# Context halves first in the last four pw1 outputs, each inverse transform one output behind its forward one, and SiLU tiles between pw2's first matmuls

## The chip, the cores and the metric

The kernel runs on one core of a Trainium2 chip. The metric is device time in microseconds; the kernel before takes 1690.03 us, the median of three runs (1689.47 to 1690.48). A core has five engines that run their own instruction streams and wait for one another through semaphores: TensorE (PE, matmuls and transposes), VectorE (DVE), ScalarE (ACT), GpSimd (POOL) and SyncE (SP), whose queue issues the weight loads here.

## The reference, cut to what matters

Two layers over 256 latent tokens and 256 context tokens of width 1024. Layer 0, the only one that the change touches, is a Conformer convolution module followed by a squared-ReLU MLP:

```
u  = x*(1+sc1) + sh1                      # sc1, sh1, g1, sc2, sh2, g2: maps of c (latent) or c_ctx
a  = u @ w_pw1 + b_pw1                    # 1024 -> 2048
a  = a[:, :1024] * sigmoid(a[:, 1024:])   # value half times gate half
a  = dwconv(a, w_dw)                      # depthwise, 31 taps; latents in rows of 64, context in one row of 256
a  = silu(layer_norm(a + b_dw))           # norm over the 1024 channels of one token
y  = a @ w_pw2 + b_pw2
h  = layer_norm(ALPHA*x + g1*y)           # LN1
h  = layer_norm(ALPHA*h + g2*sq_relu_mlp(h*(1+sc2)+sh2))
```

## The kernel before, in words

Feature-major tiles hold 128 features by 512 tokens; tokens 0 to 255 are the context (half LO, `s == 0`), 256 to 511 the latents (half HI, `s == 1`). Every fp32 product is made of three matmuls on split operands (`mm3`, lines 177, 180, 181: high by high, high by low, low by high), so a weight tile of 128x1024 is first split by ScalarE (`wh`, L154) and VectorE (`wl`, L155). The split tiles have four buffers each, the raw weights three (`raw_load`, L150, on SP's queue, in order). PSUM has eight banks: three `mm`, two `ln`, two `cv`, one `fl`.

The convolution is done as a transform. pw1's outputs come as m = 0 to 11 after four made earlier: even m is the gate of a feature tile f, odd m its value. `pw1_epi` takes a gate through Sigmoid on ScalarE (L660); for a value VectorE multiplies it in (L663), PE transposes the result (L666) and ScalarE copies it to `A` (L667), tokens on partitions. `spectral(h, tt)` makes channels 512h to 512h+511 of token block tt (0, 1 context, 2, 3 latents): forward matmuls (L683, L688), four VectorE products with the taps' spectrum (`F`, L698 and L699), then after its `yield` the inverse matmuls (L709), the bias (L716) and the statistics (L717). `token_norm(t0)` turns the statistics of blocks t0 and t0+1 into scale and shift by two aggregations and a chain of thirteen tiny VectorE operations (L722, then L507 to L512, L726 and L727) and normalizes four tiles on ScalarE (L731). `silu(s)` then makes eight tiles: two PE transposes (L751), Sigmoid and Identity on ScalarE (L754, L755), product on VectorE (L756), split (L154, L155). pw2 multiplies them; `pw2_epi` adds each output into `x` (L900) and feeds the LN1 sums (`Norm`, L433 to L462).

Beside that run the modulation maps of layer 0. `AdaRows` (`ada0`, 16 steps for g1 and sc2) makes one step of two VectorE row products (L387) on a loaded weight; `Ada` (`ada_sh`, for sh2) uses PE (L327) into the `fl` bank, a copy (L361) and a fold by PE (L335).

The instructions are put in order at build time by a scheduler that takes, engine by engine, the first ready instruction in the order of the program; those marked by `keep_in_program_order` (while `pin[0]` is true) keep their order among themselves. Before the change, m = 0 to 9 are made over 512 tokens and only m = 10, 11 in halves; the sequence around them is

```
10c 11c 10x(epi 11c) | fwd0 | 11x first half | fwd1 | 11x second half | inv0 | epi 11x | inv1
token_norm(0) | fwd2 | ada | inv2 | fwd3 | ada | inv3 | fold | silu(0) | token_norm(2) | pw2: m 0-3 kt by kt, m 4-7
```

with c and x for the context and the latent half. Then pw2 runs over the latents while `silu(1)` supplies its tiles, two for each output of the context half.

Of the kernel before, what the change touches and what calls it, by code (L numbers as in the profile page):

```python
# [72 lines left out]
def hybrid_kernel(ctx: ExitStack, tc: tile.TileContext, xT, vecs_d, rows_d, wdw_d, ada0_w, ada_w, adar_w, wg_d, pw1a, pw1, pw2, w1_0, w2_0,  # L73
# [28 lines left out]
    def psum(tag="mm"):  # L102
        return pp.tile([P, 512], F32, tag=tag, name=nm(tag), bufs={"mm": 3, "ln": 2, "fl": 1, "cv": 2}[tag])
# [44 lines left out]
    def raw_load(src):  # L148
        raw = wp.tile([P, 2048], F32, tag="raw", name=nm("raw"), bufs=3)
        nc.sync.dma_start(raw[:, :src.shape[-1]], src)  # L150
        return raw
# [113 lines left out]
        for _ in gemm2_steps(*a, **k):  # L265
            pass

    def gemm2_steps(w_ap, groups, rhs, order, epi, keep, ko=0, pre=None):


        ws = dict(pre or {})
        raws = {}

        def weights_of(m):
            if m not in ws:
                g = groups[m // 2]
                if g not in raws:
                    raws[g] = raw_load(w_ap[g, 0])
                ws[m] = split_w(raws[g][:, (m % 2) * 1024:(m % 2 + 1) * 1024], keep if m >= NW else None)
            return ws[m]  # L280

        for i, (s, sl) in enumerate(order):
            r = [(h_[:, sl], l_[:, sl]) for h_, l_ in rhs] if not isinstance(rhs, dict) else rhs[s]
            k0 = ko if i == 0 else 0
            if k0:
                pss = [psum("mm" if m < 3 else "cv")[:, :C] for m in range(k0)]
                for m in range(k0):
                    weights_of(m)
                for kt in range(8):
                    for m in range(k0):  # L290
                        mm3(pss[m], *kcol(ws[m], kt), *r[kt], kt == 0, kt == 7)
                for m in range(k0):
                    epi(m, pss[m], s, sl)
                yield
            for m in range(k0, 2 * len(groups)):
                w = weights_of(m)
                ps = psum()[:, :C]
                for kt in range(8):
                    mm3(ps, *kcol(w, kt), *r[kt], kt == 0, kt == 7)
                epi(m, ps, s, sl)  # L300
                yield
# [115 lines left out]
    class Norm:  # L417

        def __init__(self, n, bufs):
            self.n, self.ts, self.i = n, [], 0
            self.acc, self.k, self.s2 = bufs

        def add(self, t, pin=False):
            self.ts.append(t)
# [84 lines left out]
            nc.vector.scalar_tensor_tensor(q, q, 0.5, v, op0=ALU.mult, op1=ALU.mult)  # L511
            nc.vector.scalar_tensor_tensor(r, q, -1.5, r, op0=ALU.add, op1=ALU.mult)  # L512

    def norm_pair(make):

        b = [make() for _ in range(3)]
        return [Norm(C, [t[:, sl] for t in b]) for sl in (LO, HI)]

    def affine_half(hi, lo, src, s, ca, cb, f):

# [224 lines left out]
    def silu(s):  # L745
        for f in range(DT):
            if f % 2 == 0:
                tr = psum("ln")
            xn = tr[:, f % 2 * C:f % 2 * C + C]
            for i in range(2):  # L750
                nc.tensor.transpose(xn[:, i * P:(i + 1) * P], Y[2 * s + i][f // 4][:, f % 4 * P:f % 4 * P + P], ident)  # L751
# [3 lines left out]
            nc.scalar.activation(y, xn, AF.Identity, scale=V("cln_g", f), bias=V("cln_b", f))  # L755
            nc.vector.tensor_tensor(y, y, sg, op=ALU.mult)  # L756
            t = U(F32R)
            split(t[:, LO], t[:, HI], y)
            sact[s].append((t[:, LO], t[:, HI]))
            yield  # L760

    ada0, ada_sh = AdaRows(0, (2, 4)), Ada(6, 2)
    gb = con.tile([P, 2, DT], F32, name="gb")

    def pw1_next(m, ps):
        pw1_epi(m + KO0, ps)
        if m == 4:
            for tt in range(4):
                for _ in spectral(0, tt):
                    pass  # L770
        ada0.step((1, 2, 1, 2, 2, 2, 2, 2, 1, 1)[m])
        if m == 5:
            for s, sl in HALVES:
                nc.vector.tensor_tensor(gb[:, s, :], ad(0, s, "g1"), VA("b_pw2"), op=ALU.mult)
                for f in range(DT):
                    nc.vector.tensor_scalar(x[f][:, sl], x[f][:, sl], ALPHA, gb[:, s, f:f + 1], op0=ALU.mult, op1=ALU.add)
        if m == 7:
            taps(1)

    nc.sync.dma_start(cb, c_dr.rearrange("(o s c) -> o s c", o=1, s=2).broadcast_to([P, 2, D]))  # L780
    steps = gemm_steps(pw1, range(5), u, T, pw1_next)
    next(steps)

    bdw = padp.tile([P, D], F32, name="bdw")
# [50 lines left out]
    raw = raw_load(pw1[5, 0])
    wl2 = [split_w(raw[:, m * D:(m + 1) * D]) for m in range(2)]
    ps2 = [psum() for _ in range(2)]

    def pw1_part(m, s, kts=range(DT)):
        sl = HALVES[s][1]  # L840
        for kt in kts:
            mm3(ps2[m][:, sl], *kcol(wl2[m], kt), *[t_[:, sl] for t_ in u[kt]], kt == 0, kt == DT - 1)

    def part_epi(m, s):
        pw1_epi(10 + m + KO0, ps2[m], 2 * s, 2 * s + 2)

    pin[0] = True
    for m in range(2):
        pw1_part(m, 0)
        if m == 0:  # L850
            part_epi(0, 0)
    pw1_part(0, 1, range(4))
    part_epi(1, 0)
    pw1_part(0, 1, range(4, DT))
    part_epi(0, 1)
    pre_pw2(0)
    sp = [spectral(1, tt, banks=("mm", "fl")) for tt in range(2)]
    next(sp[0])
    pw1_part(1, 1, range(4))
    next(sp[1])  # L860
    pw1_part(1, 1, range(4, DT))
    for _ in sp[0]:
        pass
    part_epi(1, 1)
    for _ in sp[1]:
        pass
    normed = token_norm(0)
    pre_pw2(1)
    for tt in (2, 3):
        sp1 = spectral(1, tt, normed)  # L870
        next(sp1)
        ada_sh.mm()
        for _ in sp1:
            pass
    ada_sh.end()
    pin[0] = False
    for _ in silu(0):
        pass
    token_norm(2)
    close_pool()  # L880
    hp = open_pool("hidp")
    HD = maker(hp, "hid", 2 * DT)
    lnp = norm_pair(maker(hp, "ln", 3))
# [15 lines left out]
    def pw2_epi(m, ps, s, sl):  # L899
# [876 lines left out]
```

## Time and profile before

| | |
|---|---|
| median of three runs | 1690.03 us |
| the profiled execution's own time | 1691.92 us |
| its span on the core | 1690.2 us |
| mean granted TensorE clock | 0.996 |
| PE busy | 1660.0 us (98%) |
| DVE busy | 1091.3 us (65%) |
| ACT busy | 745.5 us (44%) |
| DMA queue of the weight loads | 285.44 MB, 46.5% of 16 engines |

Times inside the profile count from the start of the span. A row of the timeline gives an instruction's start, its length, engine, line, operation, output and inputs, and in brackets the idle time of that engine just before it with what ended it. Rows by windows give busy time by engine, then the granted TensorE clock, the share of the DMA engines and GB/s. Successive PE matmuls overlap by their pipeline, so the distance from start to start is what one costs.

### The profile page before, as it was taken

The page shows a single profiled execution, that of the slowest core. Times are in us where ns is not written, and L with a number is a line of the kernel's source. Part 1 is how long each engine was busy: PE and PEld are TensorE (multiplying, and loading weights), DVE is VectorE, ACT ScalarE, POOL GpSimd, SP SyncE. Part 2 cuts the span into 40 slices and gives each one's busy share as a digit, 9 for nine tenths or more (in the row PEclk, how much of TensorE's full clock was granted, in tenths as well). Part 3 has the DMA queues.
Part 4 walks back from the last instruction along what each step waited for, and adds up shares of the span by engine and source line. Part 5 has one row for each costly group of instructions (what it writes and reads, how often), then busy time and mean ns, then how long its engine had stood idle before and what let it go on. Part 6 is the DMA issues. An engine that isn't in the chain of part 4 may idle for free.

```text
span 1690.2 us, 22717 instructions
## 1 busy us (share of the span) xinstructions
PE 1660.0 (98%) x8853; PEld 1366.5 (81%) x8853; DVE 1091.3 (65%) x1964; ACT 745.5 (44%) x1206; POOL 33.5 (2%) x84
## 2 busy tenths in 40 slices
PE   8998999999999999999999999999999999999998
PEld 5765997888888998876688899888877878888886
DVE  7996896976666786763232543453387786678765
ACT  3322763232324465552232532442376574555652
POOL 0000000000000000000000000000011110000000
PEclk9999999999999999999999999999999999999999
DMA  9534216565545055567653632344355555645651
GB/s 387 206 128 181 95 51 224 199 224 199 198 176 200 26 183 171 186 222 280 232 187 108 213 143 100 113 161 150 117 193 188 189 195 207 244 171 216 246 181 47
DMA packets 60669, 301.60 MB, mean 178 GB/s; under 512 B 6067, under 2 KB 20947, under 8 KB 27153
## 3 DMA queue, kind: packets, MB, share of 16 engines
q1 hardware_dynamic: 42832, 285.44, 46.5%
q10 hardware_dynamic: 17728, 14.70, 2.6%
q8 instruction: 70, 1.15, 0.3%
q14 instruction: 39, 0.31, 0.1%
HBM read 284.37 MB, written 15.75 MB: 178 GB/s over the span
## 4 chain that ended last, share of the span: by engine, by line
PE 88%; DVE 7%; ACT 3%; issue 1%; DMA 1%; POOL 0%; SPq 0%; DVEq 0%; ACTq 0%; POOLq 0%
PE mm L177 17%; PE mm L180 16%; PE mm L181 16%; PE mm L192 4%; PE mm L1599 3%; PE mm L187 3%; PE mm L185 3%; PE mm L186 3%; PE mm L196 2%; DVE wl L155 2%; PE cv L186 2%; PE cv L187 2%; PE cv L185 2%; PE mm L1600 2%; PE fl L820 1%
## 5 line engine op out<-in xcount | busy, mean ns | idle before, releaser
L155 DVE TENSOR_TENSOR wl<-raw,wh 128x1024 fp32r<-128x1024 f32 x346 | 421.7, 1223 | 301.9 <-ACT wh L154 299.1
L154 ACT CAST wh<-raw 128x1024 fp32r<-128x1024 f32 x346 | 360.4, 1050 | 479.8 <-PE mm L180 282.4
L180 PE MATMUL mm<-u,wh 128*128 128x512 f32 (+1 forms) x832 | 297.8, 359 | 1.0 <-DVE u L533 0.5
L177 PE MATMUL mm<-u,wh 128*128 128x512 f32 (+1 forms) x704 | 249.7, 357 | 2.2 <-ACT wh L154 2.2
L181 PE MATMUL mm<-u,wl 128*128 128x512 f32 (+1 forms) x704 | 246.8, 352 | 0.8 <-DVE wl L155 0.8
L180 PEld LDWEIGHTS mm<-u,wh 128*128 128x128 f32 x832 | 158.0, 190 | 24.8 <-issue 1.8
L177 PEld LDWEIGHTS mm<-u,wh 128*128 128x128 f32 x704 | 133.1, 190 | 27.2 <-issue 5.1
L181 PEld LDWEIGHTS mm<-u,wl 128*128 128x128 f32 x704 | 133.7, 190 | 20.2 <-DVE wl L155 1.4
L177 PE MATMUL mm<-xm,wh 128*128 128x512 f32 x256 | 102.8, 402 | 0.0
L185 PE MATMUL mm<-wh,xl 128*128 128x512 f32 x256 | 101.3, 397 | 0.7 <-ACT wh L154 0.5
L186 PE MATMUL mm<-wh,xl 128*128 128x512 f32 x256 | 100.5, 392 | 0.6 <-DVE xl L155 0.6
L181 PE MATMUL mm<-xm,wl 128*128 128x512 f32 x256 | 100.3, 392 | 0.0
L187 PE MATMUL mm<-wl,xl 128*128 128x512 f32 x256 | 99.7, 394 | 0.2 <-DVE wl L155 0.2
L387 DVE CUSTOM_DVE_ANT_0 raw<-raw,cb,vecs 128x1024 f32<-128x1024 f32 x64 | 81.5, 1280 | 28.5 <-DMA raw<-adar_w 27.9
L177 PE MATMUL mm<-hid,wh 128*128 128x512 f32 (+1 forms) x256 | 93.2, 364 | 0.0
L180 PE MATMUL mm<-hid,wh 128*128 128x512 f32 (+1 forms) x256 | 92.9, 363 | 0.0
L181 PE MATMUL mm<-hid,wl 128*128 128x512 f32 (+1 forms) x256 | 92.9, 363 | 0.0
L1599 PE MATMUL mm<-x,wh 128*128 128x512 f32 x224 | 79.0, 397 | 0.0
L180 PE MATMUL mm<-qq,wh 128*128 128x272 f32 x256 | 73.9, 289 | 0.0
L177 PE MATMUL mm<-qq,wh 128*128 128x272 f32 x256 | 73.5, 288 | 0.0
L181 PE MATMUL mm<-qq,wl 128*128 128x272 f32 x256 | 73.5, 288 | 0.0
L192 PE MATMUL mm<-u,wh 128*128 128x512 f32 x192 | 68.4, 398 | 0.0
(498 smaller groups left out, 3288.8 us busy)
## 6 DMA issues: line engine op xcount, KB each, us to landing
raw<-w SPq DMA_DIRECT2D x64, 1024.0 KB, 4.9
raw<-adar_w SPq DMA_DIRECT2D x32, 1024.0 KB, 4.8
raw<-wo SPq DMA_DIRECT2D x32, 1024.0 KB, 4.8
raw<-ada_w SPq DMA_DIRECT2D x16, 1024.0 KB, 6.3
raw<-wv SPq DMA_DIRECT2D x16, 1024.0 KB, 5.4
raw<-wqT SPq DMA_DIRECT2D x16, 1024.0 KB, 5.2
raw<-wq SPq DMA_DIRECT2D x16, 1024.0 KB, 4.8
raw<-wk SPq DMA_DIRECT2D x16, 1024.0 KB, 4.8
```

The costliest lines, as they stand in the source:

```text
L154: c = nc.scalar.copy(hi, src)
L155: nc.vector.tensor_tensor(lo, src, hi.bitcast(F32), op=ALU.subtract)
L177: a = nc.tensor.matmul(ps, wh, xh, start=start, stop=False)
L180: nc.tensor.matmul(ps, wh, xl, start=False, stop=False)
L181: nc.tensor.matmul(ps, wl, xh, start=False, stop=stop)
L185: nc.tensor.matmul(ps, xh, wh, start=start, stop=False)
L186: nc.tensor.matmul(ps, xl, wh, start=False, stop=False)
L187: nc.tensor.matmul(ps, xh, wl, start=False, stop=stop)
L192: nc.tensor.matmul(ps, wh, x, start=start, stop=stop)
L196: nc.tensor.matmul(ps[:, :C], wl, x[:, :C], start=False, stop=False)
L387: nc.vector.tensor_tensor_reduce(dump, w, cb[:, s, :], 1.0, vecs[:, o:o + 1], ALU.mult, ALU.add, accum_out=ada[self.l][:, m, s:s + 1])
L1599: a = lambda stop: nc.tensor.matmul(ps, wh, u2[kt], start=kt == 0, stop=stop)
```

## The change

- pw1: m = 0 to 7 over 512 tokens; m = 8 to 11 all in halves, the four context halves first, then the four latent halves. Four split weights (`late_w`) stay live through it.
- Transforms of the second channel half: fwd0 after 8x, inv0 after 9x, fwd1 next, inv1 after 10x, then `token_norm(0)`, 11x, the first `ada_sh` matmul, the epilogue of 11x, fwd2, two SiLU tiles, inv2, fold, fwd3. The forward transforms use banks `cv` and `fl`.
- pw2's first three context outputs (four before) go kt by kt, one SiLU tile issued after each kt, the second `ada_sh` matmul after kt 2, inv3 after kt 4. The fourth output follows by itself. `ada_sh` becomes two objects of one block each, with a fold each.
- `ada0` makes nine of its 16 steps beside m = 0 to 7 (before 16 beside m = 0 to 9), five beside the late context halves and the last two after the pw2 loop.
- The scaling of `x` by ALPHA with the bias (16 operations, L776) goes from VectorE to ScalarE.
- One LN buffer (`acc`) lies in a pool of its own, opened earlier, since pw2's first outputs now come before the pool of the transform is closed. `silu(1)` is drawn three tiles an output instead of two. The transposes of `silu` are pinned while `pin[0]` is true.

```diff
-    def gemm2_steps(w_ap, groups, rhs, order, epi, keep, ko=0, pre=None):
+    def gemm2_steps(w_ap, groups, rhs, order, epi, keep, ko=0, pre=None, skip=0):
...
-            for m in range(k0, 2 * len(groups)):
+            for m in range(k0 if i else max(k0, skip), 2 * len(groups)):
...
-    ada0, ada_sh = AdaRows(0, (2, 4)), Ada(6, 2)
+    ada0, ada_sh = AdaRows(0, (2, 4)), [Ada(6, 1), Ada(7, 1)]
...
-        ada0.step((1, 2, 1, 2, 2, 2, 2, 2, 1, 1)[m])
-        if m == 5:
+        ada0.step(2 if m == 1 else 1)
+        if m == 6:
...
-                    nc.vector.tensor_scalar(x[f][:, sl], x[f][:, sl], ALPHA, gb[:, s, f:f + 1], op0=ALU.mult, op1=ALU.add)
+                    nc.scalar.activation(x[f][:, sl], x[f][:, sl], AF.Identity, scale=ALPHA, bias=gb[:, s, f:f + 1])
...
-    steps = gemm_steps(pw1, range(5), u, T, pw1_next)
+    steps = gemm_steps(pw1, range(4), u, T, pw1_next)
...
+    first4, last4 = range(4), range(4, DT)
     pin[0] = True
...
+    for m in range(8, 12):
+        pw1_part(m, 0, first4)
+        if m == 10:
+            part_epi(9, 0)
+        pw1_part(m, 0, last4)
+        if m != 9 and m != 11:
+            part_epi(m, 0)
+        ada0.step(2 if m == 8 else 1)
+    pw1_part(8, 1, first4)
+    part_epi(11, 0)
+    pw1_part(8, 1, last4)
+    part_epi(8, 1)
+    sp = [spectral(1, tt, banks=("cv", "fl")) for tt in range(4)]
+    next(sp[0])
+    pw1_part(9, 1)
+    run(sp[0])
+    part_epi(9, 1)
+    next(sp[1])
     pre_pw2(0)
...
+    pw1_part(10, 1)
+    run(sp[1])
+    token_norm(0)
+    part_epi(10, 1)
+    pw1_part(11, 1)
     pre_pw2(1)
...
+    ada_sh[0].mm()
+    part_epi(11, 1)
+    next(sp[2])
+    s0 = silu(0)
+    for _ in range(2):
+        next(s0)
+    run(sp[2])
+    ada_sh[0].end()
+    next(sp[3])
...
+    for kt in range(DT):
+        for m in range(K3):
+            mm3(ps3[m], *kcol(pre2[m], kt), *sact[0][kt], kt == 0, kt == DT - 1)
+        next(s0, None)
+        if kt == 2:
+            ada_sh[1].mm()
+        if kt == 4:
+            run(sp[3])
+    ada_sh[1].end()
+    ada0.flush()
+    for m in range(K3):
+        pw2_epi(m, ps3[m], 0, LO)
+    token_norm(2)
...
     side = silu(1)
-    for _ in gemm2_steps(pw2, range(4), sact, HALVES, pw2_epi, HD, ko=4, pre=pre2):
-        for _ in range(Z.nsilu):
+    for _ in steps2:
+        for _ in range(3):
             next(side, None)
```

More of the change, by code (lines that the diff above doesn't have):

```diff
@@ L417, in hybrid_kernel, with __init__ @@
     class Norm:
-        def __init__(self, n, bufs):
+        def __init__(self, n):
             self.n, self.ts, self.i = n, [], 0
-            self.acc, self.k, self.s2 = bufs
+            self.bufs = []
+        acc = property(lambda self: self.bufs[0])
+        k = property(lambda self: self.bufs[1])
+        s2 = property(lambda self: self.bufs[2])
         def add(self, t, pin=False):
@@ L512, in rsqrt, with norm_pair, rest @@
             nc.vector.scalar_tensor_tensor(r, q, -1.5, r, op0=ALU.add, op1=ALU.mult)
-    def norm_pair(make):
-        b = [make() for _ in range(3)]
-        return [Norm(C, [t[:, sl] for t in b]) for sl in (LO, HI)]
+    def norm_pair(*makes):
+        ns = [Norm(C) for _ in range(2)]
+        def rest(*makes):
+            for m in makes:
+                t = m()
+                for n_, sl in zip(ns, (LO, HI)):
+                    n_.bufs.append(t[:, sl])
+        rest(*makes)
+        return ns, rest
     def affine_half(hi, lo, src, s, ca, cb, f):
@@ L538, in hybrid_kernel @@
     cb = xp.tile([P, 2 * D], F32, tag="hl", name="cb").rearrange("p (s c) -> p s c", s=2)
+    lnk = open_pool("lnk")
     padp = open_pool("pads")
@@ L750, in silu @@
             for i in range(2):
-                nc.tensor.transpose(xn[:, i * P:(i + 1) * P], Y[2 * s + i][f // 4][:, f % 4 * P:f % 4 * P + P], ident)
+                pe(nc.tensor.transpose(xn[:, i * P:(i + 1) * P], Y[2 * s + i][f // 4][:, f % 4 * P:f % 4 * P + P], ident))
             yt = tmp("S")
@@ L834, in hybrid_kernel, with pw1_part @@
         pass
[L835 to L839, printed above, removed]
+    late_w = {}
+    def pw1_part(m, s, kts=range(DT), bank=None):
         sl = HALVES[s][1]
+        if kts[0] == 0:
+            late_p[m, s] = psum()
+        if m not in late_w:
+            raw = raw_load(pw1[m // 2, 0])
+            for i in range(2):
+                late_w[m + i] = split_w(raw[:, i * D:(i + 1) * D])
@@ L841, in pw1_part @@
         for kt in kts:
-            mm3(ps2[m][:, sl], *kcol(wl2[m], kt), *[t_[:, sl] for t_ in u[kt]], kt == 0, kt == DT - 1)
+            mm3(late_p[m, s][:, sl], *kcol(late_w[m], kt), *[t_[:, sl] for t_ in u[kt]], kt == 0, kt == DT - 1)
+    late_p = {}
     def part_epi(m, s):
-        pw1_epi(10 + m + KO0, ps2[m], 2 * s, 2 * s + 2)
-    pin[0] = True
[L848 to L853, printed above, removed]
@@ L854, in hybrid_kernel @@
-    pw1_part(0, 1, range(4, DT))
-    part_epi(0, 1)
-    pre_pw2(0)
[L857 to L867, printed above, removed]
-    pre_pw2(1)
[L869 to L883, printed above, removed]
+        pw1_epi(m + KO0, late_p[m, s], 2 * s, 2 * s + 2)
+    def run(g):
+        for _ in g:
+            pass
+    first4, last4 = range(4), range(4, DT)
+    pin[0] = True
+    for m in range(8, 12):
[6 more added lines that the diff above has]
+        ada0.step(2 if m == 8 else 1)
@@ L904, in pw2_epi @@
             ln1_half(s, sl)
+    hidden = []
+    lnp, rest = norm_pair(maker(lnk, "acc", 1))
+    K3 = 3
+    ps3 = [psum()[:, :C] for _ in range(K3)]
+    for kt in range(DT):
[11 more added lines that the diff above has]
+    token_norm(2)
+    pin[0] = False
+    steps2 = gemm2_steps(pw2, range(4), sact, HALVES, pw2_epi, lambda dt: hidden[0](dt), pre=pre2, skip=K3)
+    next(steps2)
+    close_pool()
+    hp = open_pool("hidp")
+    HD = maker(hp, "hid", 2 * DT)
+    hidden.append(HD)
+    LN2 = maker(hp, "ln", 2)
+    rest(LN2, LN2)
     side = silu(1)
-    for _ in gemm2_steps(pw2, range(4), sact, HALVES, pw2_epi, HD, ko=4, pre=pre2):
-        for _ in range(Z.nsilu):
+    for _ in steps2:
+        for _ in range(3):
             next(side, None)
@@ L978, in each0 @@
             ada_n.step()
-    lns = norm_pair(maker(hp, "ln", 3))
+    lns, _ = norm_pair(maker(lnk, "acc", 1), LN2, LN2)
     cab1, u1 = [], []
@@ L1006, in hybrid_kernel @@
     al = alpha_cols("ln2_g0", "ln2_b0")
+    close_pool()
     close_pool()
```

## The prediction

> **What bounds the kernel now.** I read the page first: the span, the busy time by engine, and for later the two steps of a weight split (mean ns behind the bar) and one row of the loads, whose last number is the median us from issue to landing.
>
> ```profile
> span 1690.2 us, 22717 instructions
> PE 1660.0 (98%) x8853; PEld 1366.5 (81%) x8853; DVE 1091.3 (65%) x1964; ACT 745.5 (44%) x1206; POOL 33.5 (2%) x84
> L155 DVE TENSOR_TENSOR wl<-raw,wh 128x1024 fp32r<-128x1024 f32 x346 | 421.7, 1223 | 301.9 <-ACT wh L154 299.1
> L154 ACT CAST wh<-raw 128x1024 fp32r<-128x1024 f32 x346 | 360.4, 1050 | 479.8 <-PE mm L180 282.4
> raw<-ada_w SPq DMA_DIRECT2D x16, 1024.0 KB, 6.3
> ```
>
> PE is busy 98% of the span and bounds it, so the change can earn only what PE loses around the stage that it rearranges, from pw1's last outputs to pw2's first. Next came busy time by windows over that stage, and one later window for comparison.
>
> ```profile
> 80.00:96.00 16.00, 14.90 (x48) 4.63 (x47) 15.51 (x29) 0.69 (x1) 0.00 (x0) 1.00 0.18 66
> 130.00:147.00 17.00, 17.00 (x113) 14.12 (x112) 5.91 (x12) 2.85 (x5) 0.00 (x0) 1.00 0.39 148
> 155.00:160.00 5.00, 2.12 (x10) 0.89 (x12) 3.81 (x13) 3.26 (x5) 0.00 (x0) 0.93 1.00 397
> 160.00:165.00 5.00, 5.00 (x26) 1.02 (x22) 2.76 (x5) 0.57 (x2) 0.00 (x0) 0.73 0.26 108
> 156.60:199.70 43.10, 41.03 (x295) 32.97 (x295) 35.69 (x98) 33.26 (x72) 0.00 (x0) 0.96 0.33 124
> 265.00:270.00 5.00, 3.72 (x20) 2.77 (x16) 3.55 (x5) 2.55 (x3) 0.00 (x0) 0.85 0.85 324
> ```
>
> Columns: PE, PEld, DVE, ACT, POOL busy, then the granted clock. The hole is at 155 to 160; the clock is down there and in the next window. DVE is full at 80 to 96 and nearly idle at 130 to 147. Third, PE's timeline, for each loss by itself.
>
> ```profile
> 84.52 1.10 PE L683 MATMUL mm<-A,ge 128*128 128x512 f32 x2 [0.51 <-DVE F L699]
> 89.81 2.27 PE L709 MATMUL cv<-F,tab 128*64 128x512 f32 x8 [0.20 <-DVE F L698]
> 93.56 2.18 PE L709 MATMUL cv<-F,tab 128*64 128x512 f32 x8 [0.24 <-DVE F L698]
> ...
> 129.83 0.63 PE L666 MATMUL ln<-ident,E 128*128 128x128 f32 x4 [1.13 <-DVE E L663]
> ...
> 149.12 0.44 PE L666 MATMUL ln<-ident,E 128*128 128x128 f32 x2
> 149.70 1.94 PE L709 MATMUL cv<-F,tab 128*64 128x512 f32 x8
> 151.57 1.13 PE L688 MATMUL mm<-A,tab 64*128 64x512 f32 x4
> 152.63 1.92 PE L327 MATMUL fl<-raw,cs 128*32 128x512 f32 x16
> 157.61 0.44 PE L751 MATMUL ln<-ident,u 128*128 128x128 f32 x2 [3.05 <-ACT u L731]
> 158.31 0.44 PE L751 MATMUL ln<-ident,u 128*128 128x128 f32 x2 [0.27 <-ACT u L731]
> 158.68 3.10 PE L709 MATMUL cv<-F,tab 128*64 128x512 f32 x8
> 161.71 1.61 PE L688 MATMUL mm<-A,tab 64*128 64x512 f32 x4
> 165.89 1.94 PE L709 MATMUL cv<-F,tab 128*64 128x512 f32 x8 [0.35 <-DVE F L698]
> 167.76 1.05 PE L335 MATMUL fl<-fold,F 128*128 128x4 f32 x8
> 168.68 0.42 PE L751 MATMUL ln<-ident,u 128*128 128x128 f32 x2
> 182.83 0.39 PE L177 MATMUL mm<-u,hid 128*128 128x256 f32 x1
> ```
>
> At 154.55 PE has nothing left: the statistics of inv1 must pass the norm chain on DVE and the normalization on ACT before SiLU's first transposes. Then the clock is low, and inv2 takes 3.10 where inv1 took 1.94. The DVE rows of that chain (first and last of 13), and the end of the same chain for the latents, which starts at 170.88:
>
> ```profile
> 154.17 0.17 DVE L507 TENSOR_SCALAR mw<-mv 128x2 f32<-128x2 f32 x1
> 156.53 0.17 DVE L727 TENSOR_SCALAR mw<-mw 128x2 f32<-128x2 f32 x1
> ...
> 170.88 0.16 DVE L507 TENSOR_SCALAR mw<-mv 128x2 f32<-128x2 f32 x1
> 176.48 0.16 DVE L727 TENSOR_SCALAR mw<-mw 128x2 f32<-128x2 f32 x1
> ```
>
> Undisturbed it takes 2.4 us; with other DVE work slipped between its links, 5.6. Last, rows of ACT around it, and three pieces of the chain of waits: a row product on DVE, and the price of a matmul on 512 and on 256 columns.
>
> ```profile
> 149.59 0.37 ACT L667 COPY A<-ln 128x256 f32<-128x256 f32 x1 [1.31 <-PE ln L666]
> 156.74 2.93 ACT L731 ACTIVATE u<-u,mw 128x512 f32<-128x512 f32 x4 [6.78 <-DVE mw L727]
> 160.03 0.55 ACT L755 ACTIVATE S<-ln,vecs 128x256 f32<-128x256 f32 x1
> ...
> 87.35 1.19 DVE dump L387
> 102.28 0.23 PE mm L181
> 130.81 0.12 PE mm L177
> ```
>
> **What can be recovered.** (a) The wait at 129.83, 1.13: m = 9's value was queued on DVE behind row products; now nine steps instead of 16 are made by the end of m = 7. (b) The hole, 3.05 + 0.27 = 3.32. After inv1 PE now has 11x (24 matmuls), one `ada` matmul block, two transposes and fwd2 before the first SiLU transposes. That is 2.88 + 1.92 + 0.84 + 1.06 = 6.7 us, the first 24 x 0.12, and 0.84 from the transposes' start at 149.12 to the end of the copy at 149.96. The chain needs L716 and L717 (0.6 each), 2.4 + 0.4 on DVE and two normalizations (1.5) on ACT, together 5.5. Covered, with 1.2 to spare. (c) The slow clock behind the hole: 3.10 - 1.94 and 1.61 - 1.13, 1.64 together. (d) The wait at 165.89, 0.35. (e) In the transforms of the first half, PE waits 0.51 + 0.20 + 0.24 and two inverses run 0.33 and 0.24 long: 1.52. DVE is the bound there (15.51 of 16), with row products (L387) in it, such as the one at 87.35. Two fewer steps by then (six for eight, 4.8 us of DVE) take them out; I take 1.2, ends 0 and 1.52. Sum: 1.13 + 3.32 + 1.64 + 0.35 + 1.2 = 7.6 us.
>
> **What it costs.** (1) Outputs 8 and 9 in halves: 48 matmuls of 0.23 become 96 of 0.12, which is +0.5. (2) Two folds for one: +0.92 on PE (167.76 to 168.68), +0.68 on DVE. The fold isn't pinned and can stand in the wait of (4); I take 0.5, ends 0 and 0.92. (3) A new wait: fwd2 needs 11x in `A`, and behind the pinned transposes nothing pinned is left to run. Transposes and copy are the 0.84 above, covered by inv1 before. Take 0.6, ends 0.2 and 0.84. The `ada` copy out of `fl` (0.68), which fwd2's first half also waits for, lies beside it. (4) inv2 waits for three products of 0.6 after fwd2's first half. fwd2's second half (0.5), two tiles' transposes (0.25 each) and a fold stand against 1.8: take 0.3, ends 0 and 1.3. (5) The late steps: five times two row products, 12 us, where DVE had 11 idle at 130 to 147; some run earlier in the time freed there. An urgent operation can still find a row product of 1.2 ahead of it. The 9c and 11c epilogues allow 12 matmuls (1.44), and 1.2 + 0.48 misses that by 0.25: two make 0.4, ends 0 and 1.2. Who is queued behind them is all of PE, by the pins. (6) pw2's three outputs hold all three `mm` banks, so the fourth waits for the first's accumulation on DVE: 0.3, ends 0 and 1. (7) The loop itself: four outputs took 168.68 to 182.83, 14.15 us, against 96 x 0.12 + 7 x 0.25 = 13.3. SiLU's pace sets the rest, now with three outputs a tile (1.08 + 0.25) against ACT's 0.46 + 0.46 + 0.30. The `ada` block and inv3 give SiLU 3.8 us. I take the same 0.85 lost, so no change. (8) DVE's debt. `flush` puts 4.8 us of row products behind the loop, and with the copy DVE has 35.69 + 5.5 = 41.2 us where it had 35.69 of 43.1. The weights of pw2's last four outputs, partly split during the loop before, now come after inv3. So `silu(1)` ends later; in the trace it ended at 200.1, 17.3 us after pw2's fifth output began (182.83), and only four context outputs of 2.88 lay between:
>
> ```profile
> 199.37 0.75 DVE L155 TENSOR_TENSOR u<-S,u 128x256 fp32r<-128x256 f32 x2
> ```
>
> PE did not idle (41.03 of the 43.1 us, the rest lost before 170): with three banks it runs several outputs over the tiles that are there. Take 0.8, ends 0 and 6.8.
>
> The scaling of `x` on ACT, 16 operations of about 0.55 (the row at 160.03), or 9 us, costs nothing: ACT is busy 0.69 of 16 us at 80 to 96. Uncovered, it would hold back a weight split. SP's queue: the loads of the late row weights, pw2's weights and `ada` keep three buffers in turn; the second `ada` block waits for the split of pw2's fourth weight, 2.3 us after 11x ends at the earliest (L154, a cast of 1.05, a subtraction of 1.22), then for a landing of 6.3 and a second megabyte behind it, 2.6 at the 397 GB/s of 155 to 160: 11.2. PE needs it after 1.92 + 0.84 + 1.06 + 0.5 + 0.3 + 1.87 + 0.92 + 1.06 + 3 x 1.33 = 12.5. In time, so nothing; ends 0 and 1.5.
>
> Costs: 0.5 + 0.5 + 0.6 + 0.3 + 0.4 + 0.3 + 0.8 = 3.4. Net 7.6 - 3.4 = 4.2 us. The stages behind (PE full from 170 on, its next wait at 266 tied to a load that PE's own progress releases) only move earlier. The profiled execution took 1691.92 us (span 1690.2 and 1.7 around it), 1.9 above the median of 1690.03, so it would become 1687.7, and the median 1685.8.
>
> **Rivals.** First, *the chain isn't covered*. pw2's weight splits and a late row product slip between its links as at 170.88 to 176.48: 5.6 for 2.4, or 8.7 against the cover of 6.7. PE waits 2.0, and the slow clock (c) is back: 4.2 - 2.0 - 1.64 = 0.6 gained, 1689.4. For it: that is how the second chain ran, and no order holds other work back from it. Against it: DVE has few ready operations then.
>
> Second, *the slow clock comes back behind small waits*. (3) and (4) leave a stretch of short matmuls and waits. The trace shows one such: a wait of 1.28 with a fold behind it, and the clock at 0.85 in the window from 265.
>
> ```profile
> 266.71 0.50 PE L177 MATMUL mm<-u,wh 128*128 128x512 f32 x1 [1.28 <-ACT wh L154]
> 267.29 0.95 PE L335 MATMUL fl<-fold,F 128*128 128x4 f32 x8
> ```
>
> Then (c) is not recovered: 1687.4. Against it: the wait of 1.13 at 129.83 was followed by clock 1.00 (130 to 147). [...]
>
> Third, on the other side, *DVE's debt starves pw2's latent half*. At the utilization of before (35.69 of 43.1) 41.2 us of DVE work take 49.8 from fwd2's products, while PE's own work from there to the latent half is 5.7 up to the loop (the same terms), 15.3 in it (8 x 1.33 + 0.85 + 1.92 + 1.87) and five outputs of 2.88: 35.4. Of the 14.4 PE can fill 7.6 (three banks, seven tiles, 0.36 each). The rest, 6.8, is a wait, and 1.64 of slow clock follows: 4.2 + 0.8 - 6.8 - 1.64 = -3.4, 1693.4. It decides once DVE ends `silu(1)` more than 12.6 us after PE wants it (7.6 filled and 5.0 of gain eaten). Against it: much of the time from 157 DVE waited for ACT, which it need not do while it flushes.
>
> **How the numbers follow.** The forecast has 0.52, the uncovered chain 0.17, the clock 0.14, the debt 0.17. The forecast's own range, from its terms' ends, is 1682.8 (all recovered, only (1) and 0.2 of (3) paid) to 1688. About 0.2% (3.4 us) is what a measurement of this kernel can tell. Faster by that (below 1686.6) is most of the forecast and a little of the clock case: 0.50; slower (above 1693.4) the worse half of the debt: 0.10; between 0.40. The range of 8 in 10 reaches from all recovered, 1682.5, to the start of the debt, 1692.
>
> **What would show it.** Right: no wait of over 1.5 us on PE between pw1's eighth output and pw2's fifth; clock 1.00 there; inv2 at 1.94; about 4 us less from 116.9 to pw2's latent half; no row product inside the first transforms. Wrong: SiLU's first transposes waiting for L731; L709 over 2.5; PE waiting for SiLU's split as the latent half of pw2 begins; L387 between L507 and L727.

## The result, and the profile after

The change made the kernel slower: 1704.28 us (median; 1701.02 to 1707.64) against 1690.15 (1689.47 to 1690.48), ratio 1.0084 with a 95% interval of 1.0057 to 1.0111. The forecast was 1685.8, with 1682.5 to 1692.0 as its range.

The page of the changed kernel, span and TensorE's line, for the profiled execution of 1707.42 us:

```profile
span 1705.7 us, 22835 instructions
PE 1671.6 (98%) x8909; PEld 1376.1 (81%) x8909; DVE 1089.0 (64%) x1951; ACT 753.8 (44%) x1224; POOL 33.4 (2%) x84
```

PE is as full as before (98%), yet 11.6 us longer busy with 56 matmuls more, 48 for the halves and 8 for the second fold. Those are priced at 0.5 + 0.9, so most of the 11.6 is the same work taking longer. Busy time by windows shows where (columns as before: PE, PEld, DVE, ACT, POOL, then the granted clock):

```profile
80.00:96.00 16.00, 14.68 (x48) 4.44 (x46) 15.47 (x28) 8.22 (x18) 0.00 (x0) 1.00 0.26 97
118.40:125.20 6.80, 6.80 (x25) 5.10 (x25) 0.85 (x2) 1.37 (x2) 0.00 (x0) 0.51 0.80 304
162.60:169.40 6.80, 6.80 (x13) 1.93 (x14) 3.05 (x6) 2.17 (x5) 0.00 (x0) 0.50 0.49 204
190.00:196.80 6.80, 6.22 (x29) 6.23 (x30) 4.63 (x15) 0.00 (x0) 0.00 (x0) 0.50 0.42 154
```

Three stretches have half the clock, each 6.827 us long by the clock records of the trace. Before, such a stretch was 3.413 us long in this part of the kernel (159.3 to 162.7). They begin at 118.26, 162.63 and 189.94, so 44.37 and 27.31 us apart, 13.0 and 8.0 times 3.413: within this trace the clock changes on a fixed grid, for whole spans of it. The first window is the first half's transforms: DVE is as full there (15.47 of 16) as before.

PE's timeline of the changed kernel, its waits of 0.2 us or more from 116 us to pw2's fifth output (the last row), one half-speed inverse among them:

```profile
116.97 0.66 PE L679 MATMUL ln<-ident,E 128*128 128x128 f32 x4 [1.47 <-DVE E L676]
158.75 0.66 PE L701 MATMUL fl<-A,tab 64*128 64x512 f32 x1 [0.82 <-DVE mw L516]
160.68 0.33 PE L764 MATMUL ln<-ident,u 128*128 128x128 f32 x1 [0.37 <-ACT u L744]
161.23 1.05 PE L335 MATMUL fl<-fold,F 128*128 128x2 f32 x8 [0.22 <-DVE F L712]
162.54 2.01 PE L701 MATMUL fl<-A,tab 64*128 64x512 f32 x2 [0.26 <-DVE ada L366]
165.10 3.68 PE L722 MATMUL cv<-F,tab 128*64 128x512 f32 x8
174.23 0.38 PE L177 MATMUL mm<-u,wh 128*128 128x256 f32 x1 [0.95 <-ACT u L154]
186.18 0.38 PE L177 MATMUL mm<-u,wh 128*128 128x256 f32 x1 [0.21 <-ACT u L154]
187.77 0.39 PE L180 MATMUL mm<-u,wh 128*128 128x256 f32 x1 [1.20 <-DVE u L155]
190.58 0.58 PE L177 MATMUL mm<-u,wh 128*128 128x256 f32 x1 [1.59 <-DVE x L922]
195.86 0.41 PE L177 MATMUL mm<-u,hid 128*128 128x256 f32 x1
```

The hole of 3.05 is gone; the nine waits of this stage make 7.09 us together. Before, the four that the prediction shows behind 116 us and one more made 5.24:

```profile
170.01 0.39 PE L180 MATMUL mm<-u,wh 128*128 128x256 f32 x1 [0.44 <-DVE u L155]
```

What DVE did ahead of the longest three, by its timeline: row products (L387) stand ahead of m = 7's value, of the last SiLU tile's second half (L155), and of pw2's first accumulation (L922).

```profile
114.96 1.28 DVE L387 CUSTOM_DVE_ANT_0 dump<-raw,cb,vecs 128x1024 bf16<-128x1024 f32 x1
116.17 0.75 DVE L676 SCALAR_TENSOR_TENSOR E<-mm,vecs,E 128x512 f32<-128x512 f32 x1
...
186.09 1.28 DVE L387 CUSTOM_DVE_ANT_0 dump<-raw,cb,vecs 128x1024 bf16<-128x1024 f32 x1
187.29 0.42 DVE L155 TENSOR_TENSOR u<-S,u 128x256 fp32r<-128x256 f32 x1
187.63 1.28 DVE L387 CUSTOM_DVE_ANT_0 raw<-raw,cb,vecs 128x1024 f32<-128x1024 f32 x1
188.83 1.28 DVE L387 CUSTOM_DVE_ANT_0 dump<-raw,cb,vecs 128x1024 bf16<-128x1024 f32 x1
190.04 0.48 DVE L922 SCALAR_TENSOR_TENSOR x<-mm,ada,x 128x256 f32<-128x256 f32 x1
```

The same line L387 by windows (DVE's busy time in it, clock, DMA), first of before, then of after:

```profile
96.00:118.00 22.00, 8.72 (x13) 1.00 0.41 148
118.00:160.00 42.00, 7.62 (x14) 0.99 0.50 187
160.00:200.00 40.00, 0.00 (x0) 0.97 0.28 103
```

```profile
96.00:118.00 22.00, 11.48 (x19) 1.00 0.42 147
118.00:160.00 42.00, 1.25 (x2) 0.92 0.25 91
160.00:200.00 40.00, 5.07 (x8) 0.83 0.38 146
```

The late steps did not run late. Those of the late context halves ran ahead of m = 7's value or right behind it, the last row product from 117.96 to 119.24; DVE then had no row product until the flush at 186.

**Where the time went.** Pw2's fifth output began at 182.83 before and at 195.86 after: 13.0 us later. Half of the halved time is lost, an estimate that takes PE as busy through it and its work as taking twice as long (inverse 2 took 3.68 here and 1.94 at clock 1.00 in the kernel before with its hole filled, below): (6.8 + 6.8 + 5.9) / 2 = 9.7 against 3.4 / 2 = 1.7, so 8.0. Waits: 7.09 - 5.24 = 1.9. The halves and the second fold: 0.5 + 0.9 = 1.4. The first half's transforms: 14.90 - 14.68 = 0.2. Together 11.5; the other 1.5 I can't assign to rows, and waits within a halved span are counted in part twice. Another 2.8 is lost behind that point, up to a matmul of the latents' LN1 sums: it starts at 213.99 before (L441) and at 229.82 after (L445), 15.8 later. 1.1 of the 2.8 is three waits for the latents' SiLU tiles and a weight, 0.39 + 0.38 + 0.31, between 206 and 208.4.

### The profile page after: what moved, and what is told of

Read it like the earlier page. It is cut to its first block, busy times and chain, and to the rows that moved or that the text cites. A ratio compares the mean times of both kernels' runs of the same rounds, so it can differ in the third digit from the quotient of the medians.

```text
span 1705.7 us, 22835 instructions
## 1 busy us (share of the span) xinstructions
PE 1671.6 (98%) x8909; PEld 1376.1 (81%) x8909; DVE 1089.0 (64%) x1951; ACT 753.8 (44%) x1224; POOL 33.4 (2%) x84
## 4 chain that ended last, share of the span: by engine, by line
PE 89%; DVE 6%; ACT 3%; issue 1%; DMA 1%; POOL 0%; SPq 0%; DVEq 0%; ACTq 0%; POOLq 0%
PE mm L177 17%; PE mm L180 16%; PE mm L181 16%; PE mm L192 4%; PE mm L1649 3%; PE mm L187 3%; PE mm L185 3%; PE mm L186 3%; PE mm L196 2%; DVE wl L155 2%; PE mm L1650 2%; PE cv L187 2%; PE cv L185 2%; PE cv L186 2%; PE fl L833 1%
## 5 line engine op out<-in xcount | busy, mean ns | idle before, releaser
L155 DVE TENSOR_TENSOR wl<-raw,wh 128x1024 fp32r<-128x1024 f32 x346 | 422.3, 1224 | 313.2 <-ACT wh L154 310.9
L180 PE MATMUL mm<-u,wh 128*128 128x512 f32 (+1 forms) x856 | 304.3, 356 | 1.9 <-DVE u L155 1.2
L177 PE MATMUL mm<-u,wh 128*128 128x512 f32 (+1 forms) x728 | 257.4, 356 | 4.4 <-DVE x L922 1.9
L181 PE MATMUL mm<-u,wl 128*128 128x512 f32 (+1 forms) x728 | 255.0, 351 | 0.8 <-DVE wl L155 0.8
L180 PEld LDWEIGHTS mm<-u,wh 128*128 128x128 f32 x856 | 165.0, 193 | 24.7 <-DVE u L155 2.1
L177 PEld LDWEIGHTS mm<-u,wh 128*128 128x128 f32 x728 | 140.2, 193 | 33.3 <-issue 7.0
L181 PEld LDWEIGHTS mm<-u,wl 128*128 128x128 f32 x728 | 140.7, 193 | 19.6 <-issue 1.6
L387 DVE CUSTOM_DVE_ANT_0 raw<-raw,cb,vecs 128x1024 f32<-128x1024 f32 x64 | 81.6, 1283 | 22.1 <-DMA raw<-adar_w 21.5
```

The source lines that it names most:

```text
L155: nc.vector.tensor_tensor(lo, src, hi.bitcast(F32), op=ALU.subtract)
L177: a = nc.tensor.matmul(ps, wh, xh, start=start, stop=False)
L180: nc.tensor.matmul(ps, wh, xl, start=False, stop=False)
L181: nc.tensor.matmul(ps, wl, xh, start=False, stop=stop)
L387: nc.vector.tensor_tensor_reduce(dump, w, cb[:, s, :], 1.0, vecs[:, o:o + 1], ALU.mult, ALU.add, accum_out=ada[self.l][:, m, s:s + 1])
```

## The experiments

Theory one in most of them: the transforms and SiLU are where the change says, and what costs is DVE work put in front of what PE needs, and the slow clock that the waits bring. Ratios are against the kernel before on the same chip, at 1689.7 to 1690.3; "less" compares medians.

**The changed kernel again** (nothing edited).

> The changed kernel once more, to see its two levels (about 1701 and 1707.5 us) on one chip. Theory one, the clock: waits of 1 to 2 us and stretches of transposes, short matmuls and folds make the gate halve TensorE's clock, in windows of 3.4 us on a grid that falls otherwise in each run; then the execution profiled here, if it is of the faster level, shows at least 3 us less of halved clock than the 24 us of the first trace, and the same waits. Theory two, VectorE's debt: the clock windows are the same and the waits of PE differ by several us.

Measured: 1703.94 us (1702.79 to 1705.55), ratio 1.0079 [1.0066, 1.0093]. In its windows:

```profile
118.00:125.00 7.00, 7.00 (x55) 6.44 (x54) 0.66 (x3) 1.67 (x3) 0.00 (x0) 1.00 0.81 300
157.00:163.80 6.80, 6.32 (x18) 3.14 (x20) 2.90 (x8) 3.36 (x7) 0.00 (x0) 0.53 0.73 305
184.00:190.80 6.80, 5.20 (x28) 5.00 (x26) 5.71 (x14) 0.00 (x1) 0.00 (x0) 0.56 0.31 102
```

The waits were the same (1.46 us for m = 7's value at 116.07), but no slow clock followed the first. A wait puts the clock at risk; whether it falls differs between executions. The scatter of 6.6 us between the changed kernel's runs fits that: a pair of slow spans costs 3.4. The two profiled executions lie 4.6 us apart, of which 3.4 is that pair; 0.9 is there before it (116.97 against 116.07).

The place of the grid sorts the three traces with this wait in which it can be read. With spans of 3.413 us counted from each trace's halved ones, the clock fell where the span ended 1.3 us behind the wait (118.26 - 116.97, the first trace of the changed kernel), so that the wait, four transposes and some of the matmuls on 31 rows behind them lay in one span. It did not fall where the span ended 0.4 (this run) or 0.9 us (no flush) behind the wait. With the 26 matmuls below it fell as well (0.55 from 118 to 125). That is one wait in a few executions, and no run moved the grid.

**No flush** (the late steps make all row products).

```diff
-        ada0.step(2 if m == 8 else 1)
+        ada0.step(1 if m == 11 else 2)
```

> The last two row-product steps go from behind pw2's loop into the late context halves (2, 2, 2, 1 steps), so nothing is flushed behind the loop. Theory one: the waits at the loop's end (0.21 + 1.20 + 1.59 us, behind row products on VectorE) and the 6.8 us of halved clock behind them (3.4 us) go, 6 us less than the changed kernel, about 1698 where that takes 1704. Theory two, VectorE is short of time over the whole stage: the work comes back as another wait and less than 1.5 us is won.

Measured: 1697.07 us, ratio 1.0044 [1.0031, 1.0057]; 6.9 us less than the changed kernel, where 6 was expected. Of the three waits at the loop's end the longest is gone and two are left, 0.20 and 0.68 for 0.21 and 1.20, with no slow clock behind them (1.00 from 167 to 253):

```profile
183.76 0.38 PE L177 MATMUL mm<-u,wh 128*128 128x256 f32 x1 [0.20 <-ACT u L154]
184.82 0.38 PE L180 MATMUL mm<-u,wh 128*128 128x256 f32 x1 [0.68 <-DVE u L155]
```

So the flush, 4.8 us of DVE work at that place, was about half of the loss (6.9 of 13.6).

**m = 7's epilogue later** (behind output 8's first half, and `taps(1)` one output earlier).

```diff
+        if m == 7:
+            held.append(ps)
+        else:
+            pw1_epi(m + KO0, ps)
-        pw1_epi(m + KO0, ps)
...
+        if m == 8:
+            pw1_epi(7 + KO0, held[0])
```

> The epilogue of pw1's output m = 7 moves behind the first half of 8c, and the taps' matmuls of the second channel half to m = 6. Theory one: the wait of 1.47 us at 115.5 and the 6.7 us of halved clock behind it go, 4.9 us less than the changed kernel, about 1699. Theory two: the row products that run ahead hold up the next value, so a wait of over 1 us stands at 8c or 10c and less than 1.5 us is won.

Measured: 1700.39 us, ratio 1.006 [1.0048, 1.0073]; 3.5 less, where 4.9 was expected. The wait is gone, and none took its place at the next outputs. The clock is 1.00 there, as it also was in one execution with the wait, so this trace alone doesn't show what the clock's part of the 3.5 is. The other two halved pairs stay (the first is shown), and a span of 3.4 from 204.4 is halved too (0.57 from 204 to 208):

```profile
118.00:125.00 7.00, 7.00 (x61) 7.00 (x60) 2.46 (x3) 1.90 (x3) 0.00 (x0) 1.00 0.79 302
156.00:163.00 7.00, 6.33 (x17) 3.25 (x19) 3.40 (x8) 3.88 (x8) 0.00 (x0) 0.54 0.77 322
```

**Both of them.**

> Both edits. Theory one: the two add, 11 us less than the changed kernel, about 1693, with one pair of slow windows left, at the latent transforms. Theory two: no more than 3 us in all.

Measured: 1695.97 us, ratio 1.0035 [1.0021, 1.0049]; 8.0 less, not the 11 expected, and less than 6.9 + 3.5. I read this as both saving slow spans that an execution has or has not; the runs' scatter (1693.5 to 1698.1) doesn't settle it.

**Another bank for tile 2's forward transform**, on top of both.

```diff
-    sp = [spectral(1, tt, banks=("cv", "fl")) for tt in range(4)]
+    sp = [spectral(1, tt, banks=("cv", "mm" if tt == 2 else "fl")) for tt in range(4)]
```

> From the kernel of the third run's kind with no flush and m = 7's epilogue later (1695.97): tile 2's forward transform takes the banks cv and mm in place of cv and fl. Theory one (the wait of 0.82 us ahead of that transform is one for the ada block's copy out of the bank fl, and not for the copy into A, as I had it): the wait falls to 0 to 0.3 and the time by 0.5 us, or by 2 us where the halved clock behind it goes too. Rival (the wait is the copy into A, 0.84 behind the transposes): no change, 1696.

Measured: 1693.30 us, ratio 1.0019 [1.001, 1.0027]; 2.7 less. PE's timeline of the kernel without this edit, then with it:

```profile
154.50 0.67 PE L701 MATMUL fl<-A,tab 64*128 64x512 f32 x1 [0.82 <-DVE mw L516]
```

```profile
153.52 0.69 PE L701 MATMUL mm<-A,tab 64*128 64x512 f32 x1 [0.46 <-ACT A L680]
```

The wait was for the `ada` block's copy out of `fl`. It was named by the DVE link that came last (`mw`), which fwd2 doesn't use: a wait named for an operation that the waiter can't need is to be looked up. What is left, 0.46, is the wait for `A` that I had forecast.

But the waiting went elsewhere. The fold uses `fl` too, and tile 3's forward transform waits until the fold is copied out of it: 0.91 here, where the kernel without the edit waited 0.22 ahead of the fold and 0.26 behind it.

```profile
157.29 1.38 PE L701 MATMUL fl<-A,tab 64*128 64x512 f32 x2 [0.91 <-DVE ada L366]
```

From the `ada` block ahead of tile 2's transform (L327) to pw2's third k step the two traces take 17.0 and 16.6 us, with one halved span each (the mean granted clock of both executions is 0.997). So the cause of the 0.82 is shown, and where the 2.7 of the medians comes from is not.

**26 matmuls into the loop's last two waits of the changed kernel** (12 ahead of the last k step, 14 behind the loop; their results are not used).

```diff
+        if kt == DT - 1:
+            busy(12, True, False)
...
+    busy(14, False, True)
```

> The changed kernel, with 26 matmuls on 256 columns added that compute nothing that is used: 12 ahead of the last k step of pw2's loop and 14 behind the loop, where TensorE waits 1.20 and 1.59 us for VectorE. Every other engine's work stays as it is. Theory one (the two waits make the clock gate halve the clock for two spans of 3.4 us, which costs 3.4 us): the halved clock at about 184 to 197 us goes, the time falls by 3 us against the changed kernel, to about 1701; the waits become 0.0 to 0.3 as TensorE works through them. Rival (the clock there is halved by something else, such as the many weight loads or a fixed pace, or follows the loop's light work): the halved spans stay and the time is the same or up to 3 us longer, since 26 matmuls at 0.12 are 3.1 us.

Measured: 1702.74 us (1700.88 to 1703.66), ratio 1.007 [1.0057, 1.0083]. By time alone that is inconclusive: 1.2 less, within both kernels' scatter. The trace:

```profile
163.00:173.40 10.40, 10.40 (x29) 4.66 (x28) 5.46 (x11) 2.12 (x5) 0.00 (x0) 0.51 0.27 112
184.00:198.00 14.00, 14.00 (x118) 14.00 (x119) 13.64 (x36) 4.99 (x10) 0.00 (x0) 1.00 0.24 87
207.00:211.00 4.00, 3.94 (x20) 3.73 (x20) 2.65 (x7) 2.96 (x9) 0.00 (x0) 0.57 0.00 0
```

The halved spans at 184 to 197 are gone. But PE then ran into DVE's next late work, the latents' SiLU tiles, with a wait of 1.13 at 205.55 and a slow span behind it. The debt of DVE that the prediction feared at the latent half is there. I read this so that in the changed kernel the slow clock gave DVE time to pay part of it (the waits there are 0.39 + 0.38 + 0.31); that was not tried by itself.

**SiLU not interleaved** (all tiles, the second `ada` block and inverse 3 ahead of pw2's loop).

```diff
+    run(s0)
+    ada_sh[1].mm()
+    run(sp[3])
     for kt in range(DT):
...
-        next(s0, None)
-        if kt == 2:
-            ada_sh[1].mm()
-        if kt == 4:
-            run(sp[3])
```

> The changed kernel with its third part undone: all SiLU tiles of the context, the second ada block and inverse 3 run ahead of pw2's loop and not between its k steps. Theory one (the interleaving in itself is a gain, and what cost is the row products and the clock): SiLU's tiles at ACT's and VectorE's pace of some 1.3 us each leave TensorE waiting for 5 tiles, about 6 us, with another halved span or two, so 1708 to 1712, slower than the changed kernel. Rival (the interleaving in itself is what costs): 1697 to 1702, faster than the changed kernel.

Measured: 1704.53 us, ratio 1.0075 [1.0061, 1.0088], the same as the changed kernel (1703.94). Neither theory had that. The tiles do leave PE waiting:

```profile
171.55 0.66 PE L764 MATMUL ln<-ident,u 128*128 128x128 f32 x4 [1.17 <-ACT S L768]
175.01 1.11 PE L764 MATMUL ln<-ident,u 128*128 128x128 f32 x4 [2.80 <-ACT S L768]
178.22 0.69 PE L764 MATMUL ln<-ident,u 128*128 128x128 f32 x2 [2.10 <-ACT S L768]
```

These 6.1 us take the place of the loop's own waits, 0.95 + 0.21 + 1.20 + 1.59, none of which is in this trace. I read this as DVE having done its work by the time PE reaches the loop. In this kernel, with its flush, the third part of the change is worth nothing that the runs can tell.

**The order of the rest**, on top of the other bank: one `ada` sum and one fold, tile 3's forward transform ahead of inverse 2, a third SiLU tile ahead of the loop, pw2's fourth weight split inside the loop and not between the links of the norm chain.

```diff
+            if self.apart and n:
+                nc.vector.tensor_tensor(self.sb, self.sb, self.ps, op=ALU.add)
...
-    run(sp[2])
-    ada_sh[0].end()
     next(sp[3])
+    run(sp[2])
+    next(s0)
...
+        if kt == 0:
+            run(p1)
         if kt == 4:
+            ada_sh.mm()
+        if kt == 2:
             run(sp[3])
```

> The same kernel as f_bank, and with it: both ada blocks added up in SBUF and folded once behind the loop (the second fold of 0.92 and its copy go), tile 2's third forward ahead of inverse 2 with a third SiLU tile ahead of the loop, pw2's fourth weight split inside the loop at its first k step and not in the middle of the context's norm chain, inverse 3 at k step 2 and the second ada block at k step 0. Theory one (the change's idea is sound, and its loss lies in the order of VectorE's work and the clock that it costs): the cluster from 11x's end to the loop shrinks by 2 to 3 us, the loop by 1, a halved span goes with 1.7: 1688 to 1692, so same as before or faster. Rival (the interleaving itself costs, by light matmuls that wait on ScalarE and VectorE one tile at a time): 1695 or more.

Measured: 1690.02 us (1688.83 to 1692.76), ratio 0.9998 [0.9989, 1.0007]: level with before. So the change's order of outputs need not cost anything; which of these edits won the 3.3 us against the last kernel was not tried one by one.

**The hole of the kernel before, filled.** 24 unused matmuls on 256 columns behind the first `ada` block of the kernel before.

```diff
         ada_sh.mm()
+        if tt == 2:
+            busy(24)
```

> The kernel before, with 24 matmuls on 256 columns (2.9 us by 0.12 each) that compute nothing that is used put into its hole of 3.05 us behind the first ada block, ahead of inverse 2. Nothing that the hole waits for gets shorter. Theory one (TensorE's idle time is what halves the clock behind the hole): the halved span of 3.4 us at 159 goes, inverse 2 takes 1.94 and not 3.10, and the time falls by 1.6 us, to about 1688.7. Rival (the clock there follows from something else, such as the transposes and folds that come next): the halved span stays and the time stays at 1690.3 or is some tenths above.

Measured: 1687.78 us (1687.06 to 1690.07), ratio 0.999 [0.9981, 0.9998]. More work and nothing removed, and 2.2 us less. PE's timeline, then a window of this kernel and the same one of before:

```profile
154.36 3.12 PE L873 MATMUL ln<-u,wh 128*128 128x256 f32 x24
157.49 0.33 PE L751 MATMUL ln<-ident,u 128*128 128x128 f32 x1
158.67 1.94 PE L709 MATMUL cv<-F,tab 128*64 128x512 f32 x8
```

```profile
268.00:273.00 5.00, 5.00 (x23) 4.14 (x23) 3.06 (x3) 3.37 (x5) 0.00 (x0) 1.00 0.94 356
```

```profile
268.00:273.00 5.00, 5.00 (x18) 3.96 (x18) 3.50 (x4) 1.99 (x2) 0.00 (x0) 0.66 0.98 390
```

Inverse 2 takes 1.94 and not 3.10, and the clock from 160 to 165 is 1.00 and not 0.73. This is the cleanest proof here that idle PE time cost its clock: the first SiLU transposes start where they did (157.49, before 157.61), and the wait is only filled. The later slow span went too, in this execution, where the wait ahead of it was shorter (0.52 for 1.28); with it the two profiled executions differ by 4.1, the medians by 2.2.

**ACT's order**, on top of the rearranged kernel: the normalizations for features that the first SiLU tiles don't need come behind those tiles' activations, and tile 3's forward transform between the first two tiles.

```diff
+        scale(0)
+        if later:
+            return scale
...
     next(s0)
     next(sp[3])
+    next(s0)
+    norm_hi(1)
     run(sp[2])
```

> The previous rearranged kernel (1690.02) with two orders changed: ACT makes the first two SiLU activations ahead of the two normalizations that they don't need, and the third forward transform stands between the first and the second SiLU tile. Theory one (the wait of 1.88 us ahead of the second tile is ACT's order, four normalizations of 0.7 ahead of the first Sigmoid): that wait falls below 0.5, pw2's loop starts 2 to 4 us earlier, and the time is 1687 to 1688.5, faster than before by 0.1 to 0.2%. Rival (VectorE's products for the transforms are the next bound and TensorE waits for them and for later tiles instead): within 0.5 of 1690.

Measured: 1687.80 us (1686.99 to 1690.40), ratio 0.9984 [0.9975, 0.9993], faster than before, and 2.2 less than the rearranged kernel (on another chip, where before was 0.4 slower). PE's second SiLU tile without and with the edit:

```profile
159.12 0.69 PE L767 MATMUL ln<-ident,u 128*128 128x128 f32 x2 [1.88 <-ACT S L771]
```

```profile
157.69 0.44 PE L773 MATMUL ln<-ident,u 128*128 128x128 f32 x2 [0.22 <-ACT S L777]
```

Both edits shorten this wait, the earlier activations and the transform put in front of the tile; they were not tried apart.

**Ten unused matmuls in the waits of that kernel.**

```diff
+    busy(4)
     next(sp[2])
+    busy(6)
     s0 = silu(0)
```

> The same with ten matmuls on 256 columns (1.2 us) that compute nothing that is used, 4 ahead of tile 2's forward transform and 6 ahead of the first SiLU transposes, where TensorE waits 0.46 and 0.45 us, then 0.38. Theory one (waits together with light matmuls make the clock gate halve the clock): the halved span there goes where the kernel without them has one, 1.7 to 3.4 us less, less the 0.3 that they reach past the waits. Rival (such short waits don't matter for the clock): the halved spans are the same and the time is the same or 0.3 us longer.

Measured: 1688.32 us, ratio 0.9991 [0.9982, 1.0]: no gain, 0.5 longer, within both kernels' scatter. The profile of the kernel without them had no slow span in that stage, with waits of 0.22 to 0.46 us (inverse 2 took 1.94 at 158.06, inverse 3 1.94 at 166.27): there was no slow clock to win back.

**36 unused matmuls in five waits** of the changed kernel with m = 7's epilogue later; the flush stays.

```diff
+    busy(7, lambda i: u[i][0][:, :C])
     next(sp[2])
+    busy(3, lambda i: u[i][0][:, :C])
...
+        if kt in (2, DT - 1):
+            busy(7 if kt == 2 else 12, lambda i: sact[0][i % 2][0])
...
+    busy(14, lambda i: sact[0][i % 4][0])
```

> The changed kernel with m = 7's epilogue later (1700.39) and 36 matmuls on 256 columns that compute nothing that is used, in its waits: 7 ahead of tile 2's forward transform (wait 0.82), 3 ahead of the first SiLU tile (0.38), 7 ahead of pw2's third k step (0.95), 12 ahead of its last (1.20) and 14 behind the loop (1.45). Theory one (the waits halve the clock, and that is a large part of the loss): the halved spans, 17 us in the profile without them, fall to 7 or less before 210 us, and the time falls by 3 to 5 us, to 1695 to 1697; the rest above before are the waits themselves and the added work. Rival (the loss is the row products and waits alone, the clock returns elsewhere as it did with 26 such matmuls): less than 1.5 us faster, 1699 or more.

Measured: 1696.31 us (1695.89 to 1697.33), ratio 1.0042 [1.0028, 1.0056]; 4.1 less than 1700.39, or 3.4 with each taken against before on its own chip (6.7 above it, for 10.1), with 36 matmuls more and nothing removed.

```profile
153.40:160.20 6.80, 6.19 (x34) 3.54 (x34) 5.13 (x14) 5.12 (x10) 0.00 (x0) 1.00 0.95 380
176.60:183.40 6.80, 6.80 (x60) 6.80 (x59) 6.50 (x17) 4.00 (x8) 0.00 (x0) 1.00 0.01 2
```

```profile
196.60 0.44 PE L764 MATMUL ln<-ident,u 128*128 128x128 f32 x2 [1.13 <-ACT S L768]
```

Both halved pairs are gone. The 1.13 for the latents' SiLU is there as in the kernel with 26 of them, and one slow span behind it (0.69 from 196 to 201).

**What the wait alone does not explain.** Two windows of the kept traces, the first span of a halved pair in the changed kernel, and the span ahead of the halved one in the kernel with both edits:

```profile
162.63:166.05 3.42, 3.42 (x8) 0.98 (x10) 1.45 (x3) 1.56 (x4) 0.00 (x0) 0.50 0.95 398
```

```profile
156.43:159.85 3.42, 2.94 (x15) 1.74 (x17) 2.63 (x6) 2.70 (x6) 0.00 (x0) 1.00 1.01 424
```

In the first PE waits for nothing, and the clock stays halved for another 3.4 us. In the second it waits 0.48 us in all, and the clock falls behind it (0.73 from 158 to 162); in the span before that it had waited 1.29, and the clock had stayed at 1.00 (tile 2's transforms took 0.59 at 155.0). What PE does there is transforms on 64 rows or 64 columns, transposes and, in the second, a fold on 2 columns. So the wait within a span does not sort these two; whether that work, or the span ahead, has a part in it was not shown, as no run tried either by itself. All the matmuls that filled waits were dense, 128x128 weights on 256 columns.

## Why the prediction was wrong

The step that failed is the slow clock: the forecast took the 1.64 of term (c) as won and added none for the waits that it put in. Its rival had the kind right ("the slow clock comes back behind small waits") and was given 0.14, but its price was one span at one place, 1.64. In the profiled execution it came in pairs at three places: 8.0 us net. Behind it stands a second error, in (a), (6) and (8): where DVE's row products would run, and so which waits PE would have. Term by term:

- (a), the wait of 1.13: not recovered. It came back as 1.47 at 116.97. I took the row products as bound to the step that issues them in the program. Nothing holds them there: the order of each engine is made of the first ready instructions, and the late ones ran ahead of m = 7's value. (The count was off as well: before, 14 steps were issued by m = 7 and 16 by m = 9.) For the same reason (5), late row products in 9c's and 11c's way, was 0: only 1.25 us of them lie between 118 and 160.
- (b), the hole: recovered but for 0.37 of 3.32. The norm chain did stretch as the first rival said, 4.3 us (154.62 to 158.91) for 2.4, with a weight split (156.71) and the `ada` copy between its links, but fwd2 waited through the end of it for another reason.
- (c), the slow clock behind the hole: not recovered. Inverse 2 took 3.68, more than the 3.10 before.
- (d), inverse 2's wait: recovered. It starts with no wait at 165.10.
- (4), 0.3 for a new wait of inverse 2: the size is near (0.22 + 0.26 = 0.48), the reason is not. These waits are ahead of the fold and of tile 3's transform, for the bank `fl` that fwd2, the fold and that transform use in turn.
- (e), the first half's transforms: 1.2 expected, -0.2 measured, by the same error as (a). As many row products (4.61 us of L387) lie from 80 to 96 as before (4.39).
- (1) and (2), halves and second fold: as costed, 1.4 with the fold at its full 0.92.
- (3), the wait ahead of fwd2: 0.82, at the end of its range, but from the copy that I had said "lies beside it"; freeing the bank left 0.46.
- (6) and (8), the accumulation and the debt: 0.3 and 0.8 taken; 1.59, and 1.20 + 0.21 ahead of it, measured, and a slow pair with them (its first span begins at 189.9, within the 1.59). The third rival saw DVE's debt but put it at the latent half. Most of it came earlier, because the flush's products were ready and stood on DVE ahead of the last SiLU tile and of the accumulation that frees pw2's bank. Taking the flush away gave 6.9 us. At the latent half 0.39 + 0.38 + 0.31 are left of it, and more where the loop's end is covered, as with the 26 and the 36 matmuls: 1.13 and 0.38.
- (7), the loop at no change: one wait of 0.95 for the third SiLU tile that isn't in the trace of before.

The forecast added no slow clock for its own waits, which it took at 0.3 to 0.6 us. No run shows a size of wait up to which the clock holds: beside waits of 0.22 to 0.46 us it held in the kernel with ACT's order, and behind 0.22 + 0.26 it fell in the kernel with both edits. With waits of 1.20 and 1.59 us, 1.2 us of matmuls between them, it fell to 0.50 (189.94 to 196.77), and with them filled by the 26 matmuls it was 1.00 (184 to 198). Behind the 1.47 it was 0.51 in one profiled execution of the changed kernel (118.4 to 125.2), and behind the same wait of 1.46 it was 1.00 in the other (118 to 125).

## What to carry to other kernels

Where a profile shows the granted clock falling behind a wait, price a new wait at its length plus one or two halved spans (1.7 us each here), as a risk and not as a sum, and count the clock behind a removed wait as won only if no other wait stays near it. A step that is "made later" in the program is later only if something holds it there; look where such instructions ran in the trace, not where they are written, and keep optional work, like the flush here, out of the queue of an engine that PE waits for. If a wait can't be removed and the clock falls behind it, dense matmuls on PE in it can pay: 24 useless ones made the kernel before 2.2 us faster. Where the clock was not falling, ten of them won nothing.

## What the runs showed of the hardware

The clock of TensorE was 0.50 or 1.00 in this stage, in whole spans of 3.413 us (3.413 or 6.827 by the clock records of the traces before and after). With the 26 matmuls three came in a row (0.51 from 163 to 173.4). With SiLU not interleaved PE worked at about half its pace at 175.0 to 176.1 and from 178.2 to 182.5: four transposes took 1.11 where they took 0.66 at 171.55, and the `ada` block 3.64 where it took 1.92 before. It fell behind 1.47 us of waiting in one execution (0.51) and not behind 1.46 in the next (1.00), which fits that the time of a kernel with many such waits scatters (1701.0 to 1707.6 for the changed one; 1689.5 to 1690.5 for the one before, in the first measurement). Waits of up to 0.46 us among short matmuls did not bring it down in the kernel with ACT's order (inverses of 1.94 throughout), but behind a span with 0.48 us of waiting and light work in the kernel with both edits it fell (0.73 from 158 to 162). So the waiting in one span doesn't decide by itself; how much of it, with which work beside it, it takes was not measured.
